# The first rows of x in two reads on two queues, first products of half the width, and norm_g as the first column of xT

## The chip, the cores and the metric

The kernel runs on one core of one Trainium2 chip. A core has TensorE (PE, with its weight loads PEld), VectorE (DVE), ScalarE (ACT), GpSimd (POOL) and SyncE (SP), each with its own queue of instructions, and 16 DMA engines that they share. The metric is the device time of one execution in microseconds (us); of several executions the median is taken. A profile is one execution taken by the hardware profiler; its times are counted from the first instruction.

## The reference

One layer of a transformer trunk on 512 tokens of width 2048, in float32: RMS norm, sliding-window attention (32 heads, 4 key/value heads, window 128) with a gate, then an embedding that is added through a second gate, and a final RMS norm. Cut to what matters here:

```python
hn = rmsnorm(x, norm_g[i])
q, k, v, gate = jnp.split(h @ w_in, [SWA_WIDTH, SWA_WIDTH + SWA_KV_WIDTH, SWA_WIDTH + 2 * SWA_KV_WIDTH], axis=-1)
...
x = x + y
emb = p[i] @ ple_proj[i]
g = jax.nn.sigmoid(rmsnorm(x, ple_norm[i]) @ ple_gate[i])
x = x + emb * g
return rmsnorm(x, final_g)
```

The kernel's start computes, for the first 256 query columns, all key columns and all value columns, the product of `x * norm_g` with the weights; the norm's factor per token (`rstd1`) is applied to the results later.

## The kernel before

**Precision.** Every float32 operand of a large product is split into a high part in fp32r and a low part, the rest. A product is the sum of three: high by high, high by low, low by high. `mm3` (lines 121 to 126) issues these three on TensorE.

**The start.** Contraction runs over 2048 rows of xT in 16 blocks (`KC`) of 128; the loop over `k` holds it. In each block SyncE loads `xr` (128 rows of xT, 512 tokens, and norm_g as the 513th column; line 190) and `w0` (128 rows, 768 columns of weights: keys, values, two tiles of queries; line 195). ScalarE multiplies `xr` by norm_g into `xh` (line 199), VectorE forms `xl`, the rest (line 203). ScalarE casts `w0` to its high part (line 207), VectorE subtracts for the low part (line 208). TensorE then runs 12 products for two tiles of queries and two of keys, and eight for the four tiles of values (lines 228 and 230), into eight accumulators that stay open over all 16 blocks. Tiles of the pool `start` have three buffers each, so the loads of block k + 3 wait until block k has been used.

**Block 0 differs.** Its `w0` is read in two pieces: columns 512 to 767 (the queries' weights) by a DMA that ScalarE issues as its first instruction (line 137), columns 0 to 511 by SyncE after `xr`. VectorE, not ScalarE, casts the queries' piece (lines 201, 202), and TensorE begins with six products for the queries, ordered by operand: high by high for both tiles, the weights' low part by `xh`, then the weights' high part by `xl` (line 216).

**The warm-up.** Ahead of it TensorE runs 34 products of 128 columns of ones (`WARM`, line 145), whose result is not used, while the first data are on their way; ScalarE loads its table for the square root with a dummy activation (line 141).

**What sets the order.** TensorE and SyncE issue in the order of the program's text (`manual_schedule`). ScalarE, VectorE and GpSimd are ordered by the framework. Waits between engines and for DMAs are semaphores, which the framework sets. DMAs that SyncE issues run in one queue (q1), those of ScalarE in another (q10).

After the start TensorE's stream goes on without a break through the attention, the gates, the output projection and the embedding's gate.

Of the kernel before, what the change touches and what calls it, by code (L numbers as in the profile page):

```python
# [11 lines left out]
F32 = mybir.dt.float32  # L12
# [7 lines left out]
S = 512  # L20
P = 128
# [16 lines left out]
EPS = 1e-6  # L38
MASKED = -3.0e38
TOEP = 384  # L40
WARM = 34
PAD = 32


# [11 lines left out]
def trunk_kernel(ctx: ExitStack, tc: tile.TileContext, a: dict):  # L56
    nc = tc.nc
# [22 lines left out]
    def quarter(name):  # L80
        return whole.tile([P, 4, S], F32, tag="quarter", name=name)

    def bank(name, tag):
        return others.get(tag, psum).tile([P, 512], F32, tag=tag, name=name)
# [36 lines left out]
    def mm3(ps, sh, sl, mh, ml, first, last, more=False):  # L121


        nc.tensor.matmul(ps, sh, mh, start=first, stop=False, skip_group_check=more)  # L124
        nc.tensor.matmul(ps, sh, ml, start=False, stop=False, skip_group_check=more)  # L125
        nc.tensor.matmul(ps, sl, mh, start=False, stop=last, skip_group_check=more)  # L126
# [8 lines left out]
    start_pool = pre.enter_context(tc.tile_pool(name="start", bufs=3))  # L135
    w0s = {0: start_pool.tile([P, 768], F32, tag="w0", name="w0_0")}
    nc.scalar.dma_start(w0s[0][:, 512:], a["w_first"][0][:, 512:])

    warm = const.tile([P, 1], F32, name="warm")
    nc.vector.memset(warm, 1.0)  # L140
    nc.scalar.activation(warm, warm, AF.Sqrt)
    ones = nc.const_aps.tensor(1.0, [P, P], mybir.dt.bfloat16)
    warm_ps = bank("warm_ps", "p")
    for _ in range(WARM):
        nc.tensor.matmul(warm_ps[:, :P], ones, ones, start=True, stop=True)

    xh, xl = [], []
    q_ps = {t: bank(f"qps{t}", "p") for t in range(2)}
# [6 lines left out]
    def run(gen):  # L155
        for _ in gen:
            pass

    def rsqrt_mean(out, ssq, n, nm):

        w = out.shape[-1]
        ms = const.tile([P, w], F32, name=f"ms_{nm}")
        rt = const.tile([P, w], F32, name=f"rt_{nm}")
        y = const.tile([P, w], F32, name=f"y_{nm}")
        t = const.tile([P, w], F32, name=f"t_{nm}")
        nc.vector.tensor_scalar(ms, ssq, 1.0 / n, EPS, op0=ALU.mult, op1=ALU.add)
        nc.scalar.activation(rt, ms, AF.Sqrt)
        yield
        nc.vector.reciprocal(y, rt)
        nc.vector.tensor_mul(t, y, y)  # L170
        nc.vector.tensor_mul(t, t, ms)
        nc.vector.tensor_scalar(t, t, -0.5, 1.5, op0=ALU.mult, op1=ALU.add)
        nc.vector.tensor_mul(out, y, t)
# [12 lines left out]
    for k in range(KC):  # L186
        both = start_pool.tile([P, 2, 768], F32R, tag="w0s", name=f"w0s{k}")
        wh, wl = both[:, 0], both[:, 1]
        xg = start_pool.tile([P, S + 1], F32, tag="xr", name=f"xr{k}")
        nc.sync.dma_start(xg, a["xT"][k * P : (k + 1) * P, :])  # L190
        xr, g1 = xg[:, :S], xg[:, S:]
        w0 = w0s[0] if k == 0 else start_pool.tile([P, 768], F32, tag="w0", name=f"w0_{k}")
        cuts = [slice(512, 768), slice(0, 512)] if k == 0 else [slice(0, 768)]
        for c in cuts[-1:]:
            nc.sync.dma_start(w0[:, c], a["w_first"][k][:, c])
        room = acts if k < KC // 2 else more
        h = room.tile([P, S], F32R, tag="ah", name=f"xh{k}")
        l = room.tile([P, S], F32R, tag="al", name=f"xl{k}")
        nc.scalar.mul(h, xr, g1)
        if k == 0:  # L200
            nc.vector.tensor_copy(wh[:, cuts[0]], w0[:, cuts[0]])
            nc.vector.tensor_sub(wl[:, cuts[0]], w0[:, cuts[0]], wh[:, cuts[0]].bitcast(F32))
        nc.vector.scalar_tensor_tensor(
            out=l, in0=xr, scalar=g1, in1=h.bitcast(F32), op0=ALU.mult, op1=ALU.subtract
        )
        for c in cuts[-1:]:
            nc.scalar.copy(wh[:, c], w0[:, c])
            nc.vector.tensor_sub(wl[:, c], w0[:, c], wh[:, c].bitcast(F32))
        xh.append(h)
        xl.append(l)  # L210
        f, e = k == 0, k == KC - 1
        qc = [slice(512 + t * P, 512 + (t + 1) * P) for t in range(2)]
        if f:
            for n, (sw, mx) in enumerate(((wh, h), (wl, h), (wh, l))):
                for t in range(2):
                    nc.tensor.matmul(q_ps[t], sw[:, qc[t]], mx, start=n == 0, stop=False)
        else:
            for t in range(2):
                mm3(q_ps[t], wh[:, qc[t]], wl[:, qc[t]], h, l, f, e)
        for t in range(2):  # L220
            c = slice(t * P, (t + 1) * P)
            mm3(kt_ps[t], wh[:, c], wl[:, c], h, l, f, e)
        for t in range(NB):
            c = slice(t * P, (t + 1) * P)

            for part in "hl" if f else "lh":
                if part == "h":
                    nc.tensor.matmul(v_ps[t], h[:, c], both[:, :, 256:512], start=f, stop=e, skip_group_check=True)  # L228
                else:
                    nc.tensor.matmul(  # L230
                        v_ps[t][:, :256], l[:, c], wh[:, 256:512], start=False, stop=False, skip_group_check=True
                    )
        if 3 <= k < 3 + NB:
            t = k - 3
            xn = quarter(f"xn{t}").rearrange("p k t -> p (k t)")
            nc.sync.dma_start(xn, a["x"][t * P : (t + 1) * P, :])
            nc.scalar.activation(xn, xn, AF.Square, accum_out=ssq1[:, t : t + 1])
        if k == 9:
            run(rsqrt_mean(rstd1, ssq1, D, "r1"))
            rdram = tc.dram_tile([NB, P], F32, name="rdram")  # L240
            nc.gpsimd.dma_start(rdram.rearrange("t p -> p t"), rstd1)
            nc.gpsimd.dma_start(rb, rdram.rearrange("t p -> (t p)").partition_broadcast(P))
        if k == 10:
            for h in range(GROUP):
                nc.sync.dma_start(sinkb[QB * h : QB * h + QB], a["sinks"][h].partition_broadcast(QB))
            nc.sync.dma_start(pn, a["ple_norm"])
# [78 lines left out]
    for b in range(exact, BUCKETS):  # L325
        d = np.nonzero(bk == b)[0]
        if len(d):
            lo, n = P - 1 + int(d.min()), len(d)
# [1017 lines left out]
    for n, p in enumerate(ORDER_PLE[:-1]):  # L1346
# [3 lines left out]
        for jj in range(2):  # L1350
# [17 lines left out]
            e = {}  # L1368
# [13 lines left out]
    f = ple_forms.made[4]  # L1382
# [80 lines left out]
    n = done[3]  # L1463
# [35 lines left out]
def laid_out(i):  # L1499

    f = lambda v: np.ascontiguousarray(v)
    w = np.asarray(i["swa_w_in"])[0]
    tiles = lambda v: f(v.reshape(KC, P, -1, P).transpose(2, 1, 0, 3).reshape(-1, P, KC * P))
    quads = lambda v: f(
        np.asarray(v).reshape(8, 2, P, 4, 512).transpose(3, 0, 2, 1, 4).reshape(4, 8, P, 1024)
    )
    qw = HEADS * HD
    kvw = KVH * HD
    x = np.asarray(i["x"])[0]
    cols = lambda v: f(np.asarray(v).reshape(KC, P).T)  # L1510
    return {
        "x": f(x),
        "xT": f(np.concatenate([x.T, np.asarray(i["norm_g"][0])[:, None]], axis=1)),
        "w_first": f(
            np.concatenate([w[:, qw : qw + 2 * kvw], w[:, : 2 * P]], axis=1).reshape(KC, P, 768)
        ),
        "w_q": tiles(w[:, :qw]),
        "w_gate_in": tiles(w[:, qw + 2 * kvw :]),
        "w_out": quads(np.asarray(i["swa_w_out"])[0]),
        "ple_gate": quads(np.asarray(i["ple_gate"])[0]),  # L1520
        "ple_norm": cols(i["ple_norm"][0]),
        "final_g": f(i["final_g"]),
        "rel": f(np.asarray(i["rel_bias"]).T),
        "sinks": f(np.asarray(i["swa_sinks"])[0].reshape(KVH, GROUP).T),
        "pT": f(np.asarray(i["p"])[0, 0].T.reshape(2, P, S).transpose(1, 0, 2)),
        "ple_proj": f(np.asarray(i["ple_proj"])[0]),
    }
# [16 lines left out]
```

## Time and profile before

| | us |
|---|---|
| median of 3 runs (lowest to highest) | 791.96 (791.55 to 792.16) |
| the profiled execution | 791.93 |
| its span, first to last instruction | 790.2 |
| TensorE busy in the span | 780.0 |

The profiled execution's own time is 1.7 us longer than its span; the rest lies before the first and after the last instruction. A row of the timeline gives start, duration, engine, line, operation, output and inputs, and in brackets how long the engine had been idle before it and what ended that. Matmul rows overlap, since products are pipelined: the distance between two starts is the pace, not the duration. "x4" means four instructions merged in a row.

The table of the start, block by block, in the profiled execution: TensorE's first real product begins at 5.00 us, block 1 at 9.30 us, block 2 at 13.46 us, block 3 at 17.61 us.

### The profile page before, as it was taken

To read this page: it belongs to the slowest core of one execution; us is meant where nothing else is said; L and a number is where in the kernel's file an instruction comes from. 1 tells how busy PE (TensorE), PEld (TensorE's weight loads), DVE (VectorE), ACT (ScalarE), POOL (GpSimd) and SP (SyncE) were. 2 spreads that over 40 slices of the span, in tenths; PEclk is the share of its full clock that TensorE was granted. 3 is DMA by queue.
4 is the path that set the end of the run, shared out by engine and by line. 5 is a ranking of instruction groups with operands and counts; after the bars stand their busy time and mean duration, and the time that the engine had idled before them with its cause. 6 is when DMAs were issued, how large, how long until landed. Compare 5 with 4: busy or idle time off the path is not lost.

```text
span 790.2 us, 11240 instructions
## 1 busy us (share of the span) xinstructions
PE 780.0 (99%) x3738; PEld 652.3 (83%) x3738; DVE 612.9 (78%) x1043; ACT 499.6 (63%) x1016; POOL 175.8 (22%) x382
## 2 busy tenths in 40 slices
PE   9999999999999999999999999999999999999995
PEld 8888888888888888888888888888888888888885
DVE  4445478887877788687887799999788757999886
ACT  5641376666666666565666656767679756667755
POOL 0012413554344414442243200100000120200000
PEclk9999999999999999999999999999999999999998
DMA  8781999999999998999998687997783995885433
GB/s 334 279 227 39 322 267 295 269 290 269 328 253 290 255 281 212 268 259 276 290 271 220 159 313 257 271 381 264 239 297 105 370 225 207 164 217 197 169 107 107
DMA packets 48490, 194.41 MB, mean 246 GB/s; under 512 B 7296, under 2 KB 7936, under 8 KB 42704
## 3 DMA queue, kind: packets, MB, share of 16 engines
q1 hardware_dynamic: 39456, 148.94, 53.2%
q0 software_dynamic: 8688, 44.36, 29.4%
q8 instruction: 29, 0.48, 0.3%
q10 hardware_dynamic: 288, 0.39, 0.2%
q14 instruction: 29, 0.24, 0.1%
HBM read 187.85 MB, written 70.31 MB: 327 GB/s over the span
## 4 chain that ended last, share of the span: by engine, by line
PE 98%; DMA 0%; DVE 0%; ACT 0%; issue 0%; DVEq 0%
PE gps L124 7%; PE gps L125 7%; PE gps L126 7%; PE qps L124 7%; PE qps L125 7%; PE qps L126 7%; PE o L126 6%; PE o L124 6%; PE o L125 6%; PE g L126 6%; PE g L125 6%; PE g L124 6%; PE s L401 2%; PE o L523 2%; PE vps L228 2%; PE pt L479 2%
## 5 line engine op out<-in xcount | busy, mean ns | idle before, releaser
L124 PE MATMUL gps<-xh,whi 128*128 128x512 f32 x256 | 100.7, 393 | 0.0
L125 PE MATMUL gps<-xl,whi 128*128 128x512 f32 x256 | 100.1, 391 | 0.0
L126 PE MATMUL gps<-xh,wlo 128*128 128x512 f32 x256 | 100.0, 391 | 0.0
L503 POOL TENSOR_SCALAR_AFFINE_SELECT own<-r 64x256 fp32r<-64x256 f32 x96 | 62.4, 650 | 162.3 <-ACT r L484 80.2
L113 DVE TENSOR_TENSOR wlo<-wraw,whi 128x1024 fp32r<-128x1024 f32 x60 | 73.5, 1226 | 24.7 <-ACT whi L107 23.2
L124 PE MATMUL qps<-xh,whi 128*128 128x512 f32 x224 | 87.8, 392 | 0.0
L125 PE MATMUL qps<-xl,whi 128*128 128x512 f32 x224 | 87.5, 391 | 0.0
L126 PE MATMUL qps<-xh,wlo 128*128 128x512 f32 x224 | 87.5, 390 | 0.0
L461 ACT ACTIVATE t<-t,sm 128x129 f32<-128x129 f32 x128 | 50.6, 397 | 51.2 <-DVE sm L452 47.9
L124 PE MATMUL g<-bhi,fhg 128*128 128x512 f32 x192 | 75.3, 392 | 0.0
L126 PE MATMUL g<-bhi,flg 128*128 128x512 f32 x192 | 74.9, 390 | 0.0
L125 PE MATMUL g<-blo,fhg 128*128 128x512 f32 x192 | 74.8, 389 | 0.0
L107 ACT CAST whi<-wraw 128x1024 fp32r<-128x1024 f32 x60 | 62.2, 1037 | 15.7 <-DMA wraw<-in_w_q 9.5
L689 ACT CAST bhi<-braw 128x1024 fp32r<-128x1024 f32 x44 | 46.4, 1057 | 36.1 <-PE g L126 20.5
L690 DVE TENSOR_TENSOR blo<-braw,bhi 128x1024 fp32r<-128x1024 f32 x44 | 54.1, 1229 | 18.5 <-ACT bhi L689 18.3
L690 DVE TENSOR_TENSOR blo<-ring,bhi 128x1024 fp32r<-128x1024 f32 x48 | 58.3, 1223 | 6.6 <-ACT bhi L689 6.2
L689 ACT CAST bhi<-ring 128x1024 fp32r<-128x1024 f32 x48 | 50.2, 1050 | 20.4 <-PE o L126 16.8
L126 PEld LDWEIGHTS gps<-xh,wlo 128*128 128x128 f32 x256 | 48.1, 188 | 10.5
L484 ACT CAST r<-pt 128x256 fp32r<-128x256 f32 x64 | 23.8, 372 | 51.3 <-PE pt L479 50.9
L124 PEld LDWEIGHTS gps<-xh,whi 128*128 128x128 f32 x256 | 48.1, 188 | 9.0
L125 PEld LDWEIGHTS gps<-xl,whi 128*128 128x128 f32 x256 | 48.1, 188 | 8.7
L671 POOL DMA_DIRECT2D grown<-in_ple_gate x16 | 13.7, 854 | 176.4 <-DMA grown<-ple_gate 119.8
(265 smaller groups left out, 1988.7 us busy)
## 6 DMA issues: line engine op xcount, KB each, us to landing
w_out<-in_w_out POOLq DMA_DIRECT2D x32, 512.0 KB, 8.7
wraw<-in_w_gate_in SPq DMA_DIRECT2D x32, 512.0 KB, 7.3
ring<-w_out SPq DMA_DIRECT2D x32, 512.0 KB, 5.9
wraw<-in_w_q SPq DMA_DIRECT2D x28, 512.0 KB, 8.1
braw<-in_ple_gate SPq DMA_DIRECT2D x24, 512.0 KB, 4.0
ring<-in_w_out SPq DMA_DIRECT2D x18, 512.0 KB, 4.5
w_out<-in_w_out SPq DMA_DIRECT2D x16, 512.0 KB, 9.6
w_out<-w_out SPq DMA_DIRECT2D x16, 512.0 KB, 13.6
```

What stands on the lines that cost most here:

```text
L107: nc.scalar.copy(hi, self.raw[i])
L113: nc.vector.tensor_sub(lo, raw, hi.bitcast(F32))
L124: nc.tensor.matmul(ps, sh, mh, start=first, stop=False, skip_group_check=more)
L125: nc.tensor.matmul(ps, sh, ml, start=False, stop=False, skip_group_check=more)
L126: nc.tensor.matmul(ps, sl, mh, start=False, stop=last, skip_group_check=more)
L228: nc.tensor.matmul(v_ps[t], h[:, c], both[:, :, 256:512], start=f, stop=e, skip_group_check=True)
L401: nc.tensor.matmul(s_ps[:, u, : 2 * n], st, key[:, :, first : first + n], start=True, stop=True)
L461: nc.scalar.activation(su, su, AF.Exp, bias=sm[:, u : u + 1], accum_out=sm[:, 2 + u : 3 + u])
L484: nc.scalar.copy(r[:, 0], PT[i])
L503: nc.gpsimd.affine_select(out=cols(own[places[g % 2 ^ low]]), in_=cols(r[here, low].bitcast(F32)), pattern=[[sign * QB, 2], [0, GROUP], [s ...
L689: nc.scalar.copy(hi, raw)
L690: nc.vector.tensor_sub(lo, raw, hi.bitcast(F32))
```

## The change

Block 0's `xr` is allocated ahead of the loop as `xg0` and read by two DMAs: SyncE reads norm_g and the first 256 tokens (257 columns), ScalarE the other 256 tokens, as its second instruction, behind its piece of `w0`. Its multiply into `xh` is done in two halves of 256 tokens, and the products high by high for the two query tiles are four of 256 columns instead of two of 512. `xl` is still formed in one instruction over 512 tokens. The warm-up has 33 products. norm_g moves from the last column of xT to the first, for all blocks. `mm3` for the queries passes a flag of the framework (`skip_group_check`) that sets no instruction.

```diff
-WARM = 34
+WARM = 33
...
     nc.scalar.dma_start(w0s[0][:, 512:], a["w_first"][0][:, 512:])
+
+    xg0 = start_pool.tile([P, S + 1], F32, tag="xr", name="xr0")
+    nc.sync.dma_start(xg0[:, :257], a["xT"][:P, :257])
+    nc.scalar.dma_start(xg0[:, 257:], a["xT"][:P, 257:])
...
-        xg = start_pool.tile([P, S + 1], F32, tag="xr", name=f"xr{k}")
-        nc.sync.dma_start(xg, a["xT"][k * P : (k + 1) * P, :])
-        xr, g1 = xg[:, :S], xg[:, S:]
+        if k == 0:
+            xg = xg0
+        else:
+            xg = start_pool.tile([P, S + 1], F32, tag="xr", name=f"xr{k}")
+            nc.sync.dma_start(xg, a["xT"][k * P : (k + 1) * P, :])
+        xr, g1 = xg[:, 1:], xg[:, :1]
...
-        nc.scalar.mul(h, xr, g1)
+        both_halves = (slice(0, 256), slice(256, 512))
+        for c in both_halves if k == 0 else (slice(0, 512),):
+            nc.scalar.mul(h[:, c], xr[:, c], g1)
...
-            for n, (sw, mx) in enumerate(((wh, h), (wl, h), (wh, l))):
+            for c in both_halves:
                 for t in range(2):
-                    nc.tensor.matmul(q_ps[t], sw[:, qc[t]], mx, start=n == 0, stop=False)
+                    nc.tensor.matmul(q_ps[t][:, c], wh[:, qc[t]], h[:, c], start=c.start == 0, stop=False, skip_group_check=True)
+            for sw, mx in ((wl, h), (wh, l)):
+                for t in range(2):
+                    nc.tensor.matmul(q_ps[t], sw[:, qc[t]], mx, start=False, stop=False, skip_group_check=True)
         else:
             for t in range(2):
-                mm3(q_ps[t], wh[:, qc[t]], wl[:, qc[t]], h, l, f, e)
+                mm3(q_ps[t], wh[:, qc[t]], wl[:, qc[t]], h, l, f, e, True)
...
-        "xT": f(np.concatenate([x.T, np.asarray(i["norm_g"][0])[:, None]], axis=1)),
+        "xT": f(np.concatenate([np.asarray(i["norm_g"][0])[:, None], x.T], axis=1)),
```

Where instructions stand otherwise stays as it was, on every engine. The first DMAs on SyncE's queue before:

```order
1 L190 DMA xr_146<-in_xT 128x513
2 L195 DMA w_0_95<-in_w_first 128x512
3 L190 DMA xr_178<-in_xT 128x513
4 L195 DMA w_1_180<-in_w_first 128x768
5 L190 DMA xr_209<-in_xT 128x513
```

and with the change (xr_97 is block 0's tile, w_0_95 its weights):

```order
1 L140 DMA xr_97<-in_xT 128x257
2 L202 DMA w_0_95<-in_w_first 128x512
3 L197 DMA xr_181<-in_xT 128x513
4 L202 DMA w_1_183<-in_w_first 128x768
5 L197 DMA xr_212<-in_xT 128x513
```

The first transfer has become half as wide; the order behind it is the same.

ScalarE's order, with the second read of x behind the queries' piece of w0, before:

```order
1 L137 DMA w_0_95<-in_w_first 128x256
2 L141 ACT_TABLE_LOAD
3 L141 ACTIVATE warm<-warm 128x1
4 L199 ACTIVATE xh_149<-xr_146 128x512
5 L207 CAST w0s_145<-w_0_95 128x512
```

and with the change:

```order
1 L137 DMA w_0_95<-in_w_first 128x256
2 L141 DMA xr_97<-in_xT 128x256
3 L145 ACT_TABLE_LOAD
4 L145 ACTIVATE warm<-warm 128x1
5 L208 ACTIVATE xh_149<-xr_97 128x256 x2
6 L216 CAST w0s_147<-w_0_95 128x512
```

A DMA stands ahead of the table load, and the multiply into xh has become two.

TensorE's first products, where qps is the accumulator of a tile of queries, before:

```order
69 L216 MATMUL qps_135<-xh_149,w0s_145 128x512
70 L216 MATMUL qps_136<-xh_149,w0s_145 128x512
71 L216 MATMUL qps_135<-xh_149,w0s_145 128x512
72 L216 MATMUL qps_136<-xh_149,w0s_145 128x512
73 L216 MATMUL qps_135<-xl_150,w0s_145 128x512
```

and with the change:

```order
67 L225 MATMUL qps_137<-xh_149,w0s_147 128x256
68 L225 MATMUL qps_138<-xh_149,w0s_147 128x256
69 L225 MATMUL qps_137<-xh_149,w0s_147 128x256
70 L225 MATMUL qps_138<-xh_149,w0s_147 128x256
71 L228 MATMUL qps_137<-xh_149,w0s_147 128x512
72 L228 MATMUL qps_138<-xh_149,w0s_147 128x512
73 L228 MATMUL qps_137<-xl_150,w0s_147 128x512
```

Two products of 512 columns have become four of 256; what follows stands as before.

## The prediction

> **What bounds the kernel now.** I read the busy times first, then the waits of TensorE, then its stretches, then the first microseconds in order of time.
>
> ```profile
> PE 780.0 (99%) x3738; PEld 652.3 (83%) x3738; DVE 612.9 (78%) x1043; ACT 499.6 (63%) x1016; POOL 175.8 (22%) x382
> ...
> PE warm_ps L145 <- PEq L1534: 0.8, 1, 0.8
> PE qps L216 <- ACT xh L199: 0.4, 1, 0.4
> ...
> 0.00:5.00 5.00, 3.79 (x34) 3.55 (x34) 0.63 (x3) 2.26 (x4) 0.69 (x6) 1.00 0.61 176
> 5.00:6.06 1.06, 1.06 (x5) 0.88 (x6) 1.06 (x3) 0.62 (x2) 0.00 (x0) 1.00 0.91 284
> 6.06:17.40 11.34, 11.34 (x57) 9.51 (x56) 6.78 (x9) 7.80 (x10) 0.00 (x0) 1.00 0.98 389
> ```
>
> (The last rows are stretches: length, busy us and count of PE, PEld, DVE, ACT, POOL, granted clock, DMA share, GB/s.) TensorE (PE) is busy for 780.0 of 790.2 us and has two waits in the whole kernel, both before 5.00 us. So the end moves with the moment at which the stream gets going; nothing later has room to take up or give back a shift. The change works on that start alone. Its rows, from the timeline, with TensorE's, ScalarE's (ACT), VectorE's (DVE) and the DMA issues (SPq, ACTq):
>
> ```profile
> 0.81 0.40 ACTq L137 DMA_DIRECT2D w<-in_w_first  x1
> 0.81 0.38 SPq L190 DMA_DIRECT2D xr<-in_xT  x1
> 0.85 3.79 PE L145 MATMUL warm_ps<-const-bfloat16-1.0 128*128 128x128 bf16 x34 [0.85 <-PEq L1534]
> 1.24 1.28 ACT L141 ACT_TABLE_LOAD   x1 [1.24 <-PEq L1534]
> 1.25 0.42 SPq L195 DMA_DIRECT2D w<-in_w_first  x1
> 2.53 0.20 ACT L141 ACTIVATE warm<-warm 128x1 f32<-128x1 f32 x1
> 4.23 0.72 ACT L199 ACTIVATE xh<-xr 128x512 fp32r<-128x512 f32 x1 [1.49 <-DMA xr<-in_xT]
> 4.39 0.29 DVE L201 CAST w0s<-w 128x256 fp32r<-128x256 f32 x1 [3.45 <-DMA w<-in_w_first]
> 4.72 0.43 DVE L202 TENSOR_TENSOR w0s<-w,w0s 128x256 fp32r<-128x256 f32 x1
> 4.94 0.62 ACT L207 CAST w0s<-w 128x512 fp32r<-128x512 f32 x1
> 5.00 0.77 PEld L216 LDWEIGHTS qps<-xh,w0s 128*128 128x128 f32 x4 [0.64 <-ACT xh L199]
> 5.00 1.21 PE L216 MATMUL qps<-xh,w0s 128*128 128x512 f32 x4 [0.37 <-ACT xh L199]
> 5.06 0.75 DVE L203 SCALAR_TENSOR_TENSOR xl<-xr,xh 128x512 fp32r<-128x512 f32 x1
> 5.72 0.69 DVE L208 TENSOR_TENSOR w0s<-w,w0s 128x512 fp32r<-128x512 f32 x1
> 5.84 0.33 SPq L190 DMA_DIRECT2D xr<-in_xT  x1
> 5.86 0.38 PEld L216 LDWEIGHTS qps<-xl,w0s 128*128 128x128 f32 x2
> 6.05 0.63 PE L216 MATMUL qps<-xl,w0s 128*128 128x512 f32 x2
> ```
>
> Two things are to be seen. First, the products start at 5.00 because xh ends at 4.95, and xh starts when the whole tile xr is there, at 4.21 (first row of the next fence). Second, and this decides: the four products with xh last from 5.00 to about 5.9, and the next pair, with xl, loads its weights at 5.86, just after xl ends (5.06 + 0.75 = 5.81). TensorE reaches xl with no slack to speak of. An earlier first product is worth only as much as xl comes earlier; a later xl is paid in full.
>
> **The change: when the data land.** Before, three transfers matter: xr (256.5 KB, SP's queue), the last 256 columns of w0 (128 KB, ACT's queue) and its first 512 (256 KB, second on SP's queue).
>
> ```profile
> 0.81 3.40 DMA xr<-in_xT
> ...
> w<-in_w_first SPq DMA_DIRECT2D x1, 256.0 KB, 3.7
> w<-in_w_first ACTq DMA_DIRECT2D x1, 128.0 KB, 3.6
> ...
> q1 hardware_dynamic: 96, 0.19, 60.5%
> q10 hardware_dynamic: 95, 0.10, 30.5%
> ```
>
> The first row is of the chain of waits (start, length): xr landed at 4.21. The next two give KB and time from issue to landing: 1.25 + 3.7 = 4.95 for the large part of w0 and 0.81 + 3.6 = 4.41 for the small one. The last two are packets, MB and share of the 16 engines of SP's queue (q1) and ACT's (q10) between 2.1 and 3.3 us: 96 against 95 packets. The engines take a row of one queue, then a row of the other, whatever its length. A row of xr took 0.605 x 1.2 x 16 / 96 = 0.121 us of an engine, a half-size row of w0 0.305 x 1.2 x 16 / 95 = 0.062.
>
> Now the first half of xr (128.5 KB) leads SP's queue, and its second half (128 KB) stands second in ACT's, behind the small part of w0. The 128 rows over 16 engines are 8 rows each, so the first half lands up to 8 x (0.121 - 0.062) = 0.47 us sooner, at 3.75 to 3.9 if some of that is lost to gaps (my estimate). The small part of w0, in step with it, gains about as much, and VectorE's cast and subtraction end near 4.75 in place of 5.15.
>
> The second half is the question; no row shows it. Lower bound: ahead of it and with it go 128.5 + 128 + 128 = 384.5 KB, just what xr and the small part of w0 were, landed at 4.21 and 4.41; so 4.3 if the large part of w0 gets no row in between. Upper bound: with all of it in between, 640.5 KB, landed by 4.95, and a further 0.2 because ACT's queue trailed SP's by 4.41 - 4.21: 5.15. In between, equal bytes for both queues would give 4.3 + 0.65 x 128 / 256 = 4.6. The packets say row for row: 8 rows of the second half then alternate with 8 rows of the large part of w0, and both end together. I take **4.95**, 0.74 us later than the whole xr landed before.
>
> [...]
>
> **The change: what follows on each engine.** On ScalarE (the order of its rows stands with the change) a DMA now precedes the table load. The added issue costs about 0.42 (SP's at 1.25) and pushes the table load and the dummy activation to end at 2.73 + 0.42 = 3.15, still ahead of 3.75: nothing. The multiply becomes two.
>
> ```profile
> L207 ACT CAST w0s<-w x16: 621/831/841, 4.9 to 59.9; 128x768 fp32r<-128x768 f32 x15, 128x512 fp32r<-128x512 f32 x1
> ...
> 6.00 0.72 ACT L199 ACTIVATE xh<-xr 128x512 fp32r<-128x512 f32 x1 [0.44 <-DMA xr<-in_xT]
> ...
> 6.76 0.75 DVE L203 SCALAR_TENSOR_TENSOR xl<-xr,xh 128x512 fp32r<-128x512 f32 x1 [0.35 <-ACT xh L199]
> ```
>
> A cast of 768 columns takes 0.831, of 512 0.621: 0.21 for 256 columns, so a half multiply is 0.72 - 0.21 = 0.51. First half: 3.85 to 4.36. Second: 4.97 (0.02 after landing, as before) to 5.48. VectorE starts xl 0.04 after xh ends (6.00 + 0.72, then 6.76): 5.52. It ends at 6.27, and TensorE loads weights 0.05 later (5.81, then 5.86): **6.32 in place of 5.86, +0.46 us**.
>
> On TensorE two wide products have become four half ones; the rest stands as it was.
>
> ```profile
> 773.66 0.28 PE L124 MATMUL last<-last,fhg 128*128 128x256 f32 x1
> ...
> 773.78 0.28 PE L125 MATMUL last<-low,fhg 128*128 128x256 f32 x1
> 773.90 0.28 PE L126 MATMUL last<-last,flg 128*128 128x256 f32 x1
> ...
> 7.21 0.40 PE L124 MATMUL ktps<-xh,w0s 128*128 128x512 f32 x1
> ...
> 7.44 0.39 PE L125 MATMUL ktps<-xl,w0s 128*128 128x512 f32 x1
> ```
>
> Half products follow each other after 0.12 us, full ones after 0.23, so the four cost 0.02 more than the two; hidden, since from 5.53 they and the pair with the low part of w0 take 0.24 + 0.46 and are through at 6.23, before xl. The first two run near 4.4 and fill what was idle. The dropped warm-up product (3.79 us for 34, so 0.11) only ends the warm-up sooner, at 4.53.
>
> Later steps keep their place. ScalarE's cast of w0 (line 207) runs 5.48 to 6.10, wanted by the key products at 6.28 + 0.46; VectorE's line 208 follows xl at 6.18 to 6.87 and is wanted at 6.75 + 0.46 = 7.21, the same 0.34 of slack as now. SP's next xr (issued at 5.84) waits for xl and slips to 6.30, for data that TensorE uses from 17.4 on:
>
> ```profile
> 6.28 0.19 PEld L124 LDWEIGHTS ktps<-xh,w0s 128*128 128x128 f32 x1
> ...
> 6.75 0.19 PEld L126 LDWEIGHTS ktps<-xh,w0s 128*128 128x128 f32 x1
> ...
> 9.31 0.19 PEld L125 LDWEIGHTS qps<-xl,w0s 128*128 128x128 f32 x1
> ...
> 17.38 0.19 PEld L124 LDWEIGHTS qps<-xh,w0s 128*128 128x128 f32 x1
> ```
>
> norm_g as the first column shifts every later xr by 4 bytes for ScalarE and VectorE; if that cost anything, xl of the next block, at 6.76 + 0.75, is wanted by the row at 9.31 alone. **Sum**: the profiled execution took 791.93, its span 790.2 and 1.73 around it; 791.93 + 0.46 = **792.4**. The median of three is 791.96, 0.03 above it.
>
> **The rivals.** (1) The second half lands early, at 4.3. Multiply 4.36 to 4.84, xl from 4.88: 0.18 us sooner, 791.75. For it: a gap in SP's queue between two transfers would give ACT's rows the engines. Against: 96 against 95.
>
> (2) The change does what it says: both halves there by 3.9. Then VectorE sets xl, from about 4.7: 0.36 sooner, 791.6. Against: 384.5 KB have to move first, and took until 4.2.
>
> (3) TensorE's pace, the case on the slower side. The 34 products of 128 columns came every 0.11 us, while 256 columns take 0.12 at the end: the start runs at half pace (though the clock column reads 1.00 there), and the full pace came near 5.25, after a hole of 0.37 us (the four products from 5.00 to 6.05 took 0.13 more than four times 0.23, which is 0.26 us at half pace). With the change the hole before xh's second half is about 4.85 to 5.53, 0.7 us. If that is too long, the pace stays halved until a stretch as long as the first (0.85 to 5.25) is filled again: half of 4.4 is 2.2, and 794.6 in all. It decides from the point where the hole counts as idle. Against: the early half products fill the old hole, so the idle total between 3.2 and 5.5 grows little.
>
> [...]
>
> **How the numbers follow.** Second half late (4.6 or after, +0.1 to +0.66, so 792.0 to 792.6): 0.60. Early: 0.21. As it says: 0.05. Pace lost: 0.10. Nothing of these: 0.04. What a measurement can tell from no change is 0.2%, 1.6 us, and only the pace reaches that. Faster 0.02, same 0.86, slower 0.12 (half of the unknown on each side). The three runs before went from 791.55 to 792.16, 0.4 below and 0.2 above their median. Below, the range takes rival 2 and half of that 0.4: 791.4. Above, it takes 792.6, the 0.2, and 0.4 for a pace that comes 0.8 us later than 5.25 without being lost: 793.2.
>
> **What would show it.** First product near 4.4; a hole of TensorE of some 0.7 us just behind two half products, released by xh; xh's second half starting 4.9 to 5.15; xl from 5.5; weights for the pair with xl near 6.3; then no waits to the end. A second half that starts before 4.6 refutes the row-for-row step; a spacing of 0.43 between full products after 5.6 means rival 3; a new wait after 7 us, or any stage after 17.4 that changes its length, means that I missed a mechanism.

## The result, and the profile after

| | us |
|---|---|
| before, median of 16 runs (lowest to highest) | 792.07 (791.55 to 792.51) |
| with the change, median of 16 runs | 793.54 (792.98 to 795.29) |
| ratio, with its 95% interval | 1.0023 (1.0016 to 1.0030) |
| the profiled execution with the change, and its span | 793.63, 791.9 |

The change costs 1.47 us. The 16 executions form two groups: eleven from 792.98 to 793.64, and five from 794.87 to 795.29. The kernel before has one group.

First the waits of TensorE (PE) and of its weight loads (PEld) in the profile with the change (us in total, times, longest), to be set beside those of before:

```profile
PE warm_ps L149 <- PEq L1546: 0.9, 1, 0.9
PE qps L225 <- ACT xh L208: 0.3, 1, 0.3
...
PEld qps L225 <- ACT xh L208: 0.6, 1, 0.6
PEld qps L126 <- DVE w0s L217: 0.5, 1, 0.5
```

TensorE still waits next to nothing. One wait is new, that for the weights' low part w0s in block 1. Now the start, from the timeline of the same profile; the first three rows are from its DMA view (KB, us from issue to landing):

```profile
xr<-in_xT SPq DMA_DIRECT2D x1, 128.5 KB, 2.7
w<-in_w_first ACTq DMA_DIRECT2D x1, 128.0 KB, 2.9
xr<-in_xT ACTq DMA_DIRECT2D x1, 128.0 KB, 3.6
...
1.25 0.45 ACTq L141 DMA_DIRECT2D xr<-in_xT  x1
...
3.56 0.51 ACT L208 ACTIVATE xh<-xr 128x256 fp32r<-128x256 f32 x1 [0.34 <-DMA xr<-in_xT]
...
4.29 0.88 PE L225 MATMUL qps<-xh,w0s 128*128 128x256 f32 x2
4.88 0.51 ACT L208 ACTIVATE xh<-xr 128x256 fp32r<-128x256 f32 x1 [0.81 <-DMA xr<-in_xT]
...
5.42 0.75 DVE L212 SCALAR_TENSOR_TENSOR xl<-xr,xh 128x512 fp32r<-128x512 f32 x1 [0.93 <-ACT xh L208]
...
5.44 0.63 PE L225 MATMUL qps<-xh,w0s 128*128 128x256 f32 x2 [0.27 <-ACT xh L208]
...
6.23 0.34 PEld L228 LDWEIGHTS qps<-xl,w0s 128*128 128x128 f32 x2
```

The second half of xr landed at 1.25 + 3.6 = 4.85, and the weights for the pair with xl were loaded at 6.23 in place of 5.86: 0.37 us late. That is the step as forecast. But the span is 1.7 us longer, so most of it arose later, after 6.23. Where, the timeline of TensorE shows at two marks, the first product of block 3 and the first product behind block 15; between them stand the sixth product of block 3 and the first of block 15's last four. Before:

```profile
17.61 0.40 PE L124 MATMUL qps<-xh,w0s 128*128 128x512 f32 x1
...
18.76 0.39 PE L126 MATMUL qps<-xh,w0s 128*128 128x512 f32 x1
...
70.81 0.28 PE L230 MATMUL vps<-w0s,xl 128*128 128x256 f32 x1
...
71.51 0.40 PE L124 MATMUL qps<-xh,whi 128*128 128x512 f32 x1
```

And with the change:

```profile
18.44 0.40 PE L124 MATMUL qps<-xh,w0s 128*128 128x512 f32 x1
...
19.61 0.40 PE L126 MATMUL qps<-xh,w0s 128*128 128x512 f32 x1
...
72.60 0.28 PE L242 MATMUL vps<-w0s,xl 128*128 128x256 f32 x1
...
73.30 0.39 PE L124 MATMUL qps<-xh,whi 128*128 128x512 f32 x1
```

The same 13 blocks of 20 products took 53.90 us before and 54.86 now, 4.147 and 4.220 a block, without any wait in them. The products themselves follow each other more slowly, but not all of them. Averaged over blocks 2 to 15, the 12 products of a block for queries and keys start 0.228 us apart before and 0.234 now (the first five steps of block 3 take 1.15 and 1.17); the eight for values start 0.176 apart in both (the last four steps of block 15 take 0.70 in both). The products for queries and keys load their weights from w0s; those for values load theirs from xh and xl and read w0s as the operand that streams through. Over the 15 blocks from 1 to 15 the loss is 15 x 0.073 = 1.1 us. At 73.30 the kernel is 1.8 us behind, and its span is 1.7 us longer, so nothing is added after the start. The wait in block 1 makes up the rest, 0.3.

What could slow the products? No row of the order has moved. But the tile xr0 is now allocated ahead of w0s, and one xr of 2052 bytes takes a slot of 2080. Three of them lie in front of w0s, so that in the built program w0s starts at byte 199712 of a partition, 32 past a multiple of 64, where before it started at byte 193472, a multiple of 64; xh and xl, which TensorE reads too, have not moved. This is theory A for the larger part. Theory A for the group near 795 is the forecast's third rival, the pace of TensorE.

### The profile page after: what moved, and what is told of

Same layout as the page of the kernel before. It is cut to its first block, busy times and chain, and to the rows that moved or that the text cites. A ratio compares the mean times of both kernels' runs of the same rounds, so it can differ in the third digit from the quotient of the medians.

```text
span 791.9 us, 11249 instructions
## 1 busy us (share of the span) xinstructions
PE 781.8 (99%) x3739; PEld 652.3 (82%) x3739; DVE 613.2 (77%) x1043; ACT 499.8 (63%) x1017; POOL 170.6 (22%) x382
## 4 chain that ended last, share of the span: by engine, by line
PE 98%; DMA 1%; DVE 1%; SPq 0%; ACT 0%; issue 0%; DVEq 0%
PE gps L124 7%; PE gps L125 7%; PE gps L126 7%; PE qps L126 7%; PE qps L124 7%; PE qps L125 7%; PE o L126 6%; PE o L124 6%; PE o L125 6%; PE g L126 6%; PE g L125 6%; PE g L124 5%; PE s L413 2%; PE o L535 2%; PE pt L491 2%; PE vps L240 2%
```

## The experiments

All were timed against the kernel before, in the same rounds on the same chip; its median was 791.96 in the first four, 792.10 in the next three and 791.89 in the last three.

**The change with the old places.** The tile of w0s is allocated ahead of xr0.

```diff
+    both0 = start_pool.tile([P, 2, 768], F32R, tag="w0s", name="w0s0")
     xg0 = start_pool.tile([P, S + 1], F32, tag="xr", name="xr0")
...
-        both = start_pool.tile([P, 2, 768], F32R, tag="w0s", name=f"w0s{k}")
+        both = both0 if k == 0 else start_pool.tile([P, 2, 768], F32R, tag="w0s", name=f"w0s{k}")
```

> The whole change, but the split weights of the start (w0s) are allocated ahead of xr, so that every tile lies where it lay before (w0s at multiples of 64 bytes; with the change they lie 32 bytes off). Theory A (the slower pace of the products of blocks 1 to 15, +1.07 us in the profile, comes from the 32 bytes): starts of key products 227 ns apart, and 792.4 to 792.8 in all, which leaves +0.33 of the start and perhaps +0.37 of block 1. Theory B (the pace comes from norm_g as first column, xr being read 4 bytes off) and theory C (it comes from the half products): 235 ns, and 793.5 as with the change. If some executions still stand 1.7 us above the others, that part has nothing to do with the places.

Measured: 792.22 (792.06 to 792.64, and one of eleven at 794.14), ratio 1.0005 (0.9996 to 1.0014). Its marks:

```profile
17.98 0.40 PE L124 MATMUL qps<-xh,w0s 128*128 128x512 f32 x1
...
71.89 0.40 PE L124 MATMUL qps<-xh,whi 128*128 128x512 f32 x1
```

53.91 us, the pace of before. The whole change without its side effect on the places costs 0.26 us, which this measurement can't tell from nothing; TensorE runs 0.38 later than before at 71.89, as it did at the start of block 1 already (9.68 against 9.30), so this is the late start.

**The kernel before with 32 bytes ahead of w0s, with 64 bytes, and with norm_g first.** The first two add one line, with 8 or 16 columns; the third makes two edits.

```diff
     w0s = {0: start_pool.tile([P, 768], F32, tag="w0", name="w0_0")}
+    start_pool.tile([P, 8], F32, tag="gap", name="gap")
```

```diff
-        xr, g1 = xg[:, :S], xg[:, S:]
+        xr, g1 = xg[:, 1:], xg[:, :1]
...
-        "xT": f(np.concatenate([x.T, np.asarray(i["norm_g"][0])[:, None]], axis=1)),
+        "xT": f(np.concatenate([np.asarray(i["norm_g"][0])[:, None], x.T], axis=1)),
```

> The kernel before with one unused tile of 32 bytes (three buffers, 96 bytes) ahead of w0s, nothing else. Theory A: key products 235 ns apart in blocks 1 to 15, +1.0 us, 793.1. Theories B and C: no change, 792.07.

> As the run before, with 64 bytes (192 in all): w0s is moved too, but stays at a multiple of 64. Theory A: no change, 227 ns and 792.07. Rival (any other place than the old one costs, whatever its remainder): 235 ns and 793.1.

> The kernel before with norm_g as the first column of xT, nothing else. Theory A: no change, 792.07, key products 227 ns apart. Theory B: 235 ns and 793.1.

Measured: 793.07, 791.95 and 791.99; ratios 1.0014 (1.0005 to 1.0023), 0.9998 (0.9990 to 1.0007), 1.0000 (0.9992 to 1.0009). The marks with 32 bytes:

```profile
17.70 0.40 PE L124 MATMUL qps<-xh,w0s 128*128 128x512 f32 x1
...
72.56 0.39 PE L124 MATMUL qps<-xh,whi 128*128 128x512 f32 x1
```

54.86 us, exactly that of the change, from an unused tile of 32 bytes in the kernel before. With 64 bytes the tile moves too, three times 64, and nothing is lost (791.95). So the move as such does not cost: w0s from byte 199712 (the change) or 193568 (32 bytes) on, both 32 past a multiple of 64, costs 1.1 us, and from 193472 or 193664 (64 bytes) on, both multiples of 64, nothing; the column of norm_g (791.99) and the half products (53.91 us with the old places) have no part in the pace. The four profiles with remainder 32 have the products for queries and keys 0.234 apart, the eight others 0.228 or 0.229.

The run with 64 bytes shows something else, in its waits:

```profile
PEld qps L126 <- DVE w0s L209: 0.5, 1, 0.5
```

That is the new wait of the profile with the change, in a kernel that lacks the change. Two more runs show it (norm_g first, and the first filled one below), the others don't. Behind it stands a late transfer for block 1: ScalarE got xr at 7.54 in the profile with the change, against 6.00 before and 6.15 in a second profile of the change, and at 6.98 in the run with 64 bytes; in the run with norm_g first it was w0 that came late. Two of six profiles with the split read have the wait, and two of six without it. So it comes with the execution, and belongs to the profiled 1.7 us rather than to the cost of the change. Why such a transfer is late is open.

**The idle stretch filled.** With the old places, and then with the change's own, nine products of ones between the two pairs of half products.

```diff
                     nc.tensor.matmul(q_ps[t][:, c], wh[:, qc[t]], h[:, c], start=c.start == 0, stop=False, skip_group_check=True)
+                for _ in range(9 if c.start == 0 else 0):
+                    nc.tensor.matmul(v_ps[3][:, :P], ones, ones, start=True, stop=True)
```

> As e1_old_places, with nine products of ones (128 columns, result overwritten later) between the first pair of half products and the second, where TensorE sat idle for 0.74 us. Theory A says that the executions 1.7 us above the others (5 of 16 with the change, 1 of 11 with the old places, none of 82 others) are those in which the idle stretch keeps TensorE at half pace for longer: with the hole filled none is left, all between 792.0 and 792.7, median 792.2. Rival D (they come from the second read on ACT's queue or from the half products themselves): one or two of eleven still near 794.

> The change as it is, tiles of the start in their new places, with nine products of ones between the two pairs of half products. Theory A (the places cost 1.1 us in every execution; the group near 795, 5 of 16 executions with the change, comes from the idle stretch of TensorE between the half products): the group near 795 is gone, the rest stays at 793.0 to 793.7, median 793.2. Rival D (the group has another cause): three or four of eleven near 795 again, median 793.4 or more.

Measured: 792.21 (ten of eleven from 791.82 to 792.82, one at 793.63) and 793.48 (ten from 793.19 to 793.88, one at 797.44). No execution of the second stands near 795. With 7 of 27 for the change itself (the next run is counted in), that alone could be chance, in one case of some 25. With the old places the filling shows nothing: one of eleven stands out with it and one without. And the median 793.48 is above the 793.2 expected and the 793.26 of the change in the same rounds. So these two runs do not settle what makes the upper group; the evidence is the profile of the next run and the shorter warm-ups below. The one at 797.44 happened to be the profiled one, and it has another cause, seen in its waits:

```profile
PE qps L124 <- ACT w0s L216: 2.1, 2, 1.1
PE qps L126 <- DVE w0s L217: 0.9, 2, 0.7
...
52.29 0.83 ACT L216 CAST w0s<-w 128x768 fp32r<-128x768 f32 x1 [6.16 <-DMA w<-in_w_first]
```

TensorE runs at full pace (0.23 us from the product at 7.17 to that at 7.40), but waits for the weights of two blocks near 53 and 68 us. The last row is ScalarE's, which waited 6.16 us for a transfer; the second time it was held up by a transfer of other weights, of 6.89 us. The outlier at 793.63 was not profiled, and its cause is open; the kernel before had one such in 28 as well (793.79).

**The change once more.** No edit.

> The change itself once more, to count the group near 795 beside the run without idle stretch. Theory A: about a third of the executions 1.5 to 2 us above the rest; the rest at 793.0 to 793.7. If none is found, the group belongs to the occasion and not to the change.

Measured: 793.26; nine of eleven from 793.05 to 793.69, two at 794.87 and 795.22. The profiled one was that at 794.87. Its start:

```profile
6.04 1.05 PE L228 MATMUL qps<-xh,w0s 128*128 128x512 f32 x2
...
8.60 0.63 PE L126 MATMUL ktps<-xh,w0s 128*128 128x512 f32 x1
9.02 0.50 PE L124 MATMUL ktps<-xh,w0s 128*128 128x512 f32 x1
9.36 0.40 PE L125 MATMUL ktps<-xl,w0s 128*128 128x512 f32 x1
```

Products start 0.42 or 0.43 us apart until 9.02, and the one at 9.36 is followed at 9.59: TensorE ran at half pace up to about 9.2 us. In the first profile of the change the full pace came at 5.74 (the record of the granted clock, last section). The 3.5 us between hold 8.1 products at 0.43, and each would take 0.234 at full pace, so about 1.6 us are lost. That is what an execution of the upper group looks like.

**A shorter warm-up.** The kernel before with 20, and with 30 warm-up products.

```diff
-WARM = 34
+WARM = 20
```

> The kernel before with 20 warm-up products in place of 34: the same data, the same products, but TensorE idle from about 3.0 to 5.0 us. Theory A: many or all executions 1 to 2 us above the kernel before, 793 to 794, in one or two groups. Rival D: no change, 792.0, since neither a second read nor half products are there.

> The kernel before with 30 warm-up products: the idle stretch of TensorE grows from 0.37 to about 0.8 us, near that of the change. [...] Rival (only a long stretch counts, as with 20 products): all near 792.0. Other rival (any longer stretch loses the pace always): all near 793.5.

Measured with 20: 793.59, all ten from 793.12 to 794.20. With 30: 793.54, in two groups, five from 791.71 to 792.33 and six from 793.54 to 794.00. Nothing else differs from the kernel before than how long TensorE sits idle ahead of the first real product. From the timelines, the last warm-up products and the first real ones, with 30:

```profile
2.61 1.59 PE L145 MATMUL warm_ps<-const-bfloat16-1.0 128*128 128x128 bf16 x13
...
4.88 1.20 PE L216 MATMUL qps<-xh,w0s 128*128 128x512 f32 x4 [0.68 <-ACT xh L199]
```

and with 20:

```profile
2.19 0.95 PE L145 MATMUL warm_ps<-const-bfloat16-1.0 128*128 128x128 bf16 x7
...
4.81 2.07 PE L216 MATMUL qps<-xh,w0s 128*128 128x512 f32 x4 [1.67 <-ACT xh L199]
```

The idle time in brackets counts from the modelled end of a product: a warm-up product's row lasts 0.31 us, though the next one starts 0.107 after it. To compare kernels whose products differ in width, I count from the last start plus the columns at half pace, 0.107 us for 128. The last warm-up product starts 0.31 before the end of its merged row. That gives 2.61 + 1.59 - 0.31 + 0.11 = 4.00 to 4.88, 0.88 us with 30 products, and 1.9 with 20. In the kernel before it is 0.85 + 3.79 - 0.31 + 0.11 = 4.44 to 5.00, 0.56. With the change there are two pieces. The first pair of half products begins at 4.29 and, as a narrower view shows, at 4.65:

```profile
4.65 0.52 PE L225 MATMUL qps<-xh,w0s 128*128 128x256 f32 x1
```

Each takes 0.21 at half pace, so TensorE is idle from 4.50 to 4.65 and from 4.86 to 5.44, 0.73 in all.

| idle time, us | executions in the upper group, by their time |
|---|---|
| 0.56 (before) | none of some 100, but for one at 793.79 that was not profiled |
| 0.73 (the change) | 7 of 27; with the old places 1 of 11 |
| 0.88 (30 products) | 6 of 11 |
| 1.9 (20 products) | 10 of 10 |

The share grew with the idle time in these four kernels. Both rivals about its length fail, and so does rival D: the kernel before, with neither a second read nor half products, gets the same second group. The profile with 20 products shows the late pace as well: the full clock came at 8.35, against 5.07 before.

**Both halves on SP's queue**, with the old places (allocated as above).

```diff
-    nc.scalar.dma_start(xg0[:, 257:], a["xT"][:P, 257:])
+    nc.sync.dma_start(xg0[:, 257:], a["xT"][:P, 257:])
```

> As e1_old_places, but both halves of the first rows are read on SP's queue, one behind the other, ahead of the large part of w0. Theory A (queues are served row for row, so on ACT's queue the second half shares with the large part of w0): the second half now lands near 4.2 in place of 4.97, its multiply starts near 4.25, the weights for the pair with xl are loaded near 5.6 in place of 6.33, and the median is 791.5 to 791.8, below the kernel before. Rival E (the bytes alone decide, the order does not): second half near 4.9 again, 792.2.

Measured: 792.51 (eleven from 791.96 to 792.73, one at 796.27), ratio 1.0008 (0.9999 to 1.0017). The step expected is there, the gain is not:

```profile
xr<-in_xT SPq DMA_DIRECT2D x1, 128.0 KB, 2.8
...
3.63 0.96 ACT L209 ACTIVATE xh<-xr 128x256 fp32r<-128x256 f32 x2 [0.89 <-DMA xr<-in_xT]
...
4.62 0.75 DVE L213 SCALAR_TENSOR_TENSOR xl<-xr,xh 128x512 fp32r<-128x512 f32 x1
...
5.39 1.05 PE L229 MATMUL qps<-xh,w0s 128*128 128x512 f32 x2
...
5.89 0.62 ACT L217 CAST w0s<-w 128x512 fp32r<-128x512 f32 x1 [1.30 <-DMA w<-in_w_first]
```

The second half landed near 4.05, both multiplies were done by 4.59 and xl began at 4.62, 0.8 us before the change's. Rival E is out. But in this execution TensorE worked at half pace (two products in 1.05 us, against 0.63 at 6.05 us in the kernel before), so the early data were used up slowly: it waited for nothing once the products had begun, and the full clock came only at 6.82. At full pace the large part of w0 would be the next limit, as I estimate from these times: now third in SP's queue, it landed at 5.9 in place of 4.95, and its cast ended at 6.51, later than the first load of a key's weights in the kernel before (6.28). How much each of the two takes in an average execution is open, and so is the cause of the one at 796.27. No variant tried beats the kernel before.

## Why the prediction was wrong, point by point

The forecast was 792.4, in a range from 791.4 to 793.2; measured were 793.54.

- **What bounds the kernel** held: TensorE's stream has no slack, and a shift at the start arrives at the end. With the old places 0.38 us of it is there at 71.89 us.
- **When the data land** held for the half that decides. The second half landed at 4.85 (forecast 4.95), beside the large part of w0 at 1.25 + 3.4 = 4.65; between 3.0 and 4.0 us SP's queue moved 133 packets and ACT's 121, so nearly row for row. That the order in the queue makes it late is shown by the run with both halves on SP's queue, 4.05. The first half landed at 0.81 + 2.7 = 3.5, sooner than the 3.75 to 3.9 forecast, and the small part of w0 at 3.7; neither set the time.
- **The late xl** held in size: +0.37 in the profiled weight load (+0.47 with the old places, 6.33), forecast +0.46. In the median it is 0.26 with the old places, which can't be told from nothing. The whole change with the old places, 792.22, lies inside the range.
- **norm_g as the first column** at no cost: shown.
- **"Later steps keep their place"** is the step that failed. It was argued from the order of the instructions and their waits, and both did stay. The prediction weighed the 4 bytes by which xr is read further on, and put the place of every other tile at nothing without a word. But the diff moves the allocation of xr0 ahead of w0s, and 32 bytes slowed the products that load their weights from w0s, every block of the start by 0.073 us, 1.1 us in all. The text named its own test, a stage after 17.4 us that changes its length, and that stage did.
- **The third rival** (the pace) was given 0.10 as if it took all executions or none. It takes some: 7 of 27, by 1.6 to 2.1 us (794.87 to 795.29 against 793.23) in place of the 2.2 forecast. The hole came from 4.86 to 5.44, where 4.85 to 5.53 was forecast. It lifts the median of the 16 from 793.23, that of the lower eleven, to 793.54. The prediction read a full pace from about 5.25 before; the record of the granted clock has 5.07. With 30 warm-up products the second product behind the wait started about 0.1 late although the clock had risen before, at 4.90: at 5.22, 0.34 behind the first, where later ones stand 0.23 apart.

The sum is 1.1 for the places (793.07 - 791.96) and 0.26 for the late start, 1.4 in all, to which the second group adds what it adds to a median; measured +1.47 and, the second time, +1.37. The sum closes to some 0.3 us: the lower eleven alone stand 1.16 above the kernel before.

## What to carry to other kernels

Where a diff allocates a tile earlier or later, look at the addresses of the tiles behind it as well as at the order of instructions: here an odd row length put in front of the weights cost 1.1 us, and the change itself 0.26. An early first product was of little use while TensorE ran at half pace (at 4.28 in place of 5.00 with both halves on SP's queue, where the median was 792.51), and a small piece that starts early and then waits can go with a longer stay there: of the 7 executions in 27 of the upper group one was profiled, and its full clock came at 9.24 (5.74 in the lower group). The second queue did not bring all the data sooner: between 3.0 and 4.0 us the two moved 133 and 121 packets, and the first half came at 3.5, the second at 4.85, where one read had brought the whole at 4.21 and both halves on one queue were there at 4.05.

## What the runs showed of the hardware that was not expected

With the tile of weights w0s 32 bytes past a multiple of 64, at 199712 and at 193568, the products that load their weights from it started 0.234 us apart, against 0.228 or 0.229 at a multiple of 64, for products of 512 columns. The products that stream the same tile past weights from elsewhere kept their 0.176, with the change as before. Remainders other than 0 and 32 were not tried.

TensorE's pace did not go up at one fixed moment after the kernel's start: in two profiles of the change it did at 5.74 and at 9.24 us. The trace's record of the granted clock shows when the full clock came, from 3.70 to 9.24 us in the twelve profiles, and how long it lasted: 778.24 us (before), 781.65 (the first profile of the change) or 785.07. (The record begins with that rise; for the time ahead of it there is none, and a clock column reads 1.00 there, though the warm-up products of 128 columns stand 0.107 us apart, half pace.) These lengths differ by 3.413 us and are 228, 229 and 230 times that. What sets this step was not shown.

What TensorE must have done ahead of a rise, the traces leave open in part. The table has the share of the 3.413 us ahead of the rise in which TensorE had columns to feed, counted from the starts of the products and their columns at the pace of the moment (before its first product TensorE is taken as idle), and, where the products had begun by then, the same for the 3.413 us before, at whose end the clock did not rise:

| profile | full clock at, us | 3.413 us ahead of it | the 3.413 us before |
|---|---|---|---|
| filled, old places | 3.70 | 83% | |
| before | 5.07 | 83% | 24% |
| both halves on SP's queue | 6.82 | 93% | 75% |
| 20 warm-up products | 8.35 | 95% | 45% |
| 30 warm-up products | 4.90 | 74% | 19% |
| the change | 5.74 | 76% | 43% |
| the change once more | 9.24 | 100% | 75% |

In the five profiles not listed it is 84% to 94% and at most 34%. So the full clock came after all stretches of 83% and more and after none of 45% and less, while of four stretches of 74 to 76% two were followed by it and two were not. That such a share over 3.413 us decides is my estimate from this table; if it does, the bound lies near three quarters, closer than this count can tell. The two profiles of the change stand on either side of it: in both, one stretch (2.32 to 5.74, and 2.41 to 5.82) held both idle pieces around the half products, and the clock rose at its end in the first and not in the second. That fits a second group that takes only some of the executions; for those that were not profiled it is argued, not shown.
